# The low parts of the first 56 weight tiles: GpSimd subtracts, where ScalarE negated and a DMA added

## The chip, the cores and the metric

The kernel runs on one core of one Trainium2 chip. The metric is the device time of one execution, in microseconds (us). A core has five engines with a program each: TensorE (PE; its weight loads are listed as PEld), VectorE (DVE), ScalarE (ACT), GpSimd (POOL) and SyncE (SP), which here only issues DMAs. Sixteen DMA engines are shared by all queues: q1 holds what SP issues, q0 what POOL issues.

## What is computed

The reference is a stack of four layers on a sequence of 512 tokens of width 1024, in float32: a convolution beside an RWKV recurrence, a sparse attention, a gated linear recurrence, and a full attention. Only the first lines of the first layer matter here:

```python
mod = cond @ ada_w[l] + ada_b[l]
shift, scale, gate = jnp.split(mod, 3, axis=-1)
h = rms_norm(x, norm_g[l]) * (1.0 + scale[:, None, :]) + shift[:, None, :]
z = h @ even_w_in[j]
a_val, a_glu, a_gate, r, k, v, wd, ad, b_gate = split_cols(z, EVEN_SIZES)
```

## The kernel before

**Products in three parts.** Every float32 weight w and every activation x is written as a high part in TensorE's fp32r format and a low part, the rest. A product is then three matmuls (`mm3`, lines 168 to 170): high weight by high activation, high weight by low activation, low weight by high activation. In the profile the tiles are `wr` (raw weights as loaded), `wh` and `wl` (their high and low parts); the high and low parts of the activations are both called `h`.

**How a weight is split.** `wparts` takes up to four weight tiles of 128x128 at once. ScalarE casts them into `wh` (L145) and writes their negative, rounded to fp32r, into `wl` (L146); then a DMA on POOL's queue adds the raw weights to `wl` (L147), reading and writing SBUF. The rounded negative is minus the high part, so what is left is the low part. `wr` has three buffers, `wh` and `wl` have four each.

**The first stage, called START here.** The layer begins with seven column blocks (`START`: one of each kind of output) that go through all eight input blocks k = 0 to 7 together, each in its own PSUM bank, so that the work can begin with the first input block. `wrows` (L150) loads the seven weight tiles of one k in one DMA (L155, 448 KB) and calls `wparts` twice, with four tiles and with three. That is 8 x 7 = 56 tiles, 16 calls, and nothing else calls `wrows`. Each k is 7 x 3 = 21 matmuls of 512 columns.

**The modulation beside it.** The scale and shift of two input blocks at a time come from `ada_first`, 2 MB for each pair of blocks, loaded by SP (L434) into two buffers, `AR` and `BK`. `columns` multiplies and adds it on DVE (L445, L447: eight instructions), four small matmuls sum over partitions (L450), DVE adds the bias (L453, L428), scales x (L501) and ScalarE and DVE make the two parts of `h` (L332, L333). So the matmuls of k = 2, 4 and 6 wait for an L450 group that stands in PE's own order.

**After START** come single column blocks (`project`, `wsplit`), the convolution's taps on DVE (L859, 216 instructions), and two loops over eight chunks of the recurrence (`chunk`, `ahead`), in which ScalarE copies (L733, L739, L750, L772) stand between small matmuls.

**The order** of each engine's instructions is set when the kernel is built: a scheduler runs a model of the timeline over the whole program and writes each engine's list. SP's DMAs are a list of their own and start in that order; eight semaphores go round among them, so that a DMA also waits for the one eight before it.

Of the kernel before, what the change touches and what calls it, by code (L numbers as in the profile page):

```python
# [10 lines left out]
F = mybir.dt.float32  # L11
# [4 lines left out]
OP = mybir.AluOpType  # L16
# [36 lines left out]
class Ctx:  # L53
# [84 lines left out]
            out += [(h[:, i], l[:, i]) for i in range(n)] if rows else [[z.rearrange("p a c -> p (a c)") for z in (h, l)]]  # L138
        return out

    def wparts(self, raw, tag=None):

        nc, n = self.nc, raw.shape[1]
        h, l = ((self.t(tag, (P, 4, P), R) if tag else self.wp.tile([P, 4, P], R, name=self.name(z), tag=z, bufs=4))[:, :n] for z in ("wh", "wl"))
        nc.scalar.copy(h, raw)  # L145
        nc.scalar.mul(l, raw, -1.0)  # L146
        nc.gpsimd.dma_start(out=l, in_=raw, accum_op=OP.add)  # L147
        return h, l

    def wrows(self, key, ct, k):  # L150

        nc = self.nc
        raw = self.wp.tile([P, 8, P], F, name=self.name("wr"), tag="wr", bufs=3)
        n, d = len(ct), ct[1] - ct[0]
        nc.sync.dma_start(out=raw[:, :n], in_=self.ins[key][ct[0]:ct[-1] + 1:d, :, k].rearrange("c p n -> p c n"))  # L155
        out = []
        for o in (0, 4):
            m = min(4, n - o)
            h, l = self.wparts(raw[:, o:o + m])
            out += [(h[:, i], l[:, i]) for i in range(m)]  # L160
        return out

# [1500 lines left out]
```

## Time and profile before

| | |
|---|---|
| median of 3 runs | 1786.72 us (1777.45 to 1789.82) |
| the profiled execution | 1791.05 us, its span 1789.3 us |
| busy in the span | PE 1657.9 us, DVE 1142.2, ACT 1090.4, POOL 637.6 |
| mean granted TensorE clock | 0.955 of full speed |

The times in the rows count from the start of the span. "Granted clock" is the share of full speed that TensorE was given. An idle time in brackets behind a row is that of the engine just before it, with what ended it.

### The profile page before, as it was taken

To read this page: it belongs to the slowest core of one execution; us is meant where nothing else is said; L and a number is where in the kernel's file an instruction comes from. 1 tells how busy PE (TensorE), PEld (TensorE's weight loads), DVE (VectorE), ACT (ScalarE), POOL (GpSimd) and SP (SyncE) were. 2 spreads that over 40 slices of the span, in tenths; PEclk is the share of its full clock that TensorE was granted. 3 is DMA by queue.
4 is the path that set the end of the run, shared out by engine and by line. 5 is a ranking of instruction groups with operands and counts; after the bars stand their busy time and mean duration, and the time that the engine had idled before them with its cause. 6 is when DMAs were issued, how large, how long until landed. Compare 5 with 4: busy or idle time off the path is not lost.

```text
span 1789.3 us, 26544 instructions
## 1 busy us (share of the span) xinstructions
PE 1657.9 (93%) x9250; PEld 1310.1 (73%) x9250; DVE 1142.2 (64%) x2247; ACT 1090.4 (61%) x2106; POOL 637.6 (36%) x678
## 2 busy tenths in 40 slices
PE   5899999998995999888999899999999999999997
PEld 4676777776664777767887688888788777877775
DVE  6489776795948567456968878922688621454442
ACT  3574545445554435478565678765789755776775
POOL 1244423233566212133323445332333333333332
PEclk9899997898998989899999999999999999999999
DMA  9866894446678976476879741078777798865654
GB/s 284 211 147 163 184 215 110 107 95 174 153 179 193 273 219 151 119 170 142 179 168 229 197 89 35 18 166 193 165 177 167 150 190 190 199 143 138 154 109 116
DMA packets 164087, 289.19 MB, mean 162 GB/s; under 512 B 43985, under 2 KB 60753, under 8 KB 162929
## 3 DMA queue, kind: packets, MB, share of 16 engines
q0 software_dynamic: 60352, 107.24, 35.7%
q1 hardware_dynamic: 99568, 172.91, 30.9%
q10 hardware_dynamic: 4032, 7.34, 1.1%
q8 instruction: 73, 1.20, 0.3%
q14 instruction: 62, 0.50, 0.1%
HBM read 162.10 MB, written 18.12 MB: 101 GB/s over the span
## 4 chain that ended last, share of the span: by engine, by line
PE 59%; DVE 13%; DMA 12%; issue 8%; ACT 3%; POOL 3%; SPq 1%; POOLq 0%; DVEq 0%; ACTq 0%
PE ps L168 15%; PE ps L169 15%; PE ps L170 15%; DVE x L859 4%; DMA wl<-wr 3%; DMA wr<-in_even_w_in 2%; POOL wl L147 1%; DMA adm<-in_ada_w 1%; PE ps L1525 1%; PE ps L729 1%; DMA sp<-gt 1%; PE ps L1521 1%; PE ps L550 1%; PE ps L1261 1%; POOL mean L894 1%
## 5 line engine op out<-in xcount | busy, mean ns | idle before, releaser
L147 POOL DMA_DIRECT2D wl<-wr x416 | 364.7, 882 | 871.6 <-ACT wl L146 772.3
L170 PE MATMUL ps<-h,wl 128*128 128x512 f32 x1240 | 498.8, 406 | 29.4 <-DMA wl<-wr 29.0
L168 PE MATMUL ps<-h,wh 128*128 128x512 f32 x1240 | 508.5, 415 | 18.7 <-ACT h L332 6.8
L169 PE MATMUL ps<-h,wh 128*128 128x512 f32 x1240 | 500.0, 405 | 0.1
L145 ACT CAST wh<-wr 128x512 fp32r<-128x512 f32 (+1 forms) x416 | 251.9, 606 | 355.6 <-PE ps L169 253.8
L170 PEld LDWEIGHTS ps<-h,wl 128*128 128x128 f32 x1240 | 241.0, 195 | 91.0 <-DMA wl<-wr 37.5
L168 PEld LDWEIGHTS ps<-h,wh 128*128 128x128 f32 x1240 | 243.4, 197 | 83.3 <-ACT h L332 8.3
L169 PEld LDWEIGHTS ps<-h,wh 128*128 128x128 f32 x1240 | 242.0, 195 | 52.7 <-issue 2.7
L146 ACT ACTIVATE wl<-wr 128x512 fp32r<-128x512 f32 (+1 forms) x416 | 256.5, 617 | 28.0 <-PE ps L169 26.5
L859 DVE SCALAR_TENSOR_TENSOR x<-cu,vec,x 128x512 f32<-128x512 f32 x216 | 185.9, 862 | 4.9
L1258 POOL TENSOR_SCALAR pp<-pp,st 128x512 f32<-128x512 f32 x32 | 52.2, 1632 | 68.9 <-DVE st L1254 58.8
L1253 ACT ACTIVATE pp<-pp,st 128x512 f32<-128x512 f32 x64 | 46.2, 722 | 18.2 <-DVE st L1252 18.0
L1515 DVE CUSTOM_DVE_ANT_0 pp<-ps,nb 128x128 f32<-128x128 f32 (+3 forms) x64 | 30.6, 488 | 30.3 <-PE ps L1510 21.8
L169 PE MATMUL ps<-wl,h 128*128 128x512 f32 x120 | 47.6, 398 | 0.7 <-DMA wl<-wr 0.7
L1252 DVE CUSTOM_DVE_ANT_0 pp<-ps,bias 128x512 f32<-128x512 f32 x64 | 43.6, 681 | 6.4 <-PE ps L1261 6.0
L170 PE MATMUL ps<-wh,h 128*128 128x512 f32 x120 | 46.5, 393 | 0.0
L688 DVE TENSOR_TENSOR q<-q,q 128x112 f32<-128x112 f32 (+25 forms) x108 | 27.2, 288 | 29.2 <-DMA q<-sp 28.8
L168 PE MATMUL ps<-wh,h 128*128 128x512 f32 x120 | 45.4, 405 | 0.0
L288 ACT CAST pT<-ps 128x512 fp32r<-128x512 f32 x64 | 36.4, 577 | 14.1 <-PE ps L1261 13.6
L1518 POOL TENSOR_SCALAR pp<-pp,st 128x128 f32<-128x128 f32 (+1 forms) x32 | 32.0, 1032 | 36.5 <-DVE st L1517 36.4
L289 DVE TENSOR_TENSOR pT<-ps,pT 128x512 fp32r<-128x512 f32 x64 | 43.3, 680 | 0.8 <-ACT pT L288 0.7
L1188 DVE MATCH_REPLACE8 acc<-m,acc 128x512 f32<-128x512 f32 x64 | 42.8, 674 | 0.0
(522 smaller groups left out, 3332.1 us busy)
## 6 DMA issues: line engine op xcount, KB each, us to landing
wl<-wr POOLq DMA_DIRECT2D x376, 256.0 KB, 4.1
wr<-in_even_w_in SPq DMA_DIRECT2D x50, 512.0 KB, 4.1
wr<-in_odd_w_in SPq DMA_DIRECT2D x39, 512.0 KB, 4.2
wr<-in_lru_w_in SPq DMA_DIRECT2D x24, 512.0 KB, 3.8
wr<-in_fox_w_qkg SPq DMA_DIRECT2D x24, 512.0 KB, 4.4
k<-in_ada_w SPq DMA_DIRECT2D x32, 256.0 KB, 3.9
wr<-in_odd_w_out SPq DMA_DIRECT2D x16, 512.0 KB, 4.0
wl<-wr POOLq DMA_DIRECT2D x40, 192.0 KB, 4.1
```

The lines of the kernel that those rows point to most:

```text
L145: nc.scalar.copy(h, raw)
L146: nc.scalar.mul(l, raw, -1.0)
L147: nc.gpsimd.dma_start(out=l, in_=raw, accum_op=OP.add)
L168: mm(ps, lhsT=w[0], rhs=x[0], start=first, stop=False)
L169: mm(ps, lhsT=w[0], rhs=x[1], start=False, stop=False)
L170: self.last_mm = mm(ps, lhsT=w[1], rhs=x[0], start=False, stop=last).ins
L289: nc.vector.tensor_tensor(out=l, in0=src, in1=h.bitcast(F), op=OP.subtract)
L859: nc.vector.scalar_tensor_tensor(out=acc, in0=u[:, q:q + S], scalar=w[q], in1=acc, op0=OP.mult, op1=OP.add)
L1188: nc.vector.match_replace(out=acc, in_to_replace=m8, in_values=acc, imm_value=TAKEN)
L1252: nc.vector.tensor_tensor_reduce(out=pp, in0=lg, in1=bias[t], scale=1.0, scalar=3e38, op0=OP.add, op1=OP.min, accum_out=mx)
L1253: nc.scalar.activation(pp, pp, AF.Exp, scale=-1.0, bias=mx, accum_out=sm)
L1258: (nc.vector if t % 2 else nc.gpsimd).tensor_scalar(out=pp, in0=pp, scalar1=sm, scalar2=None, op0=OP.mult)
```

## The change

`wparts` gets a switch `sub`, and `wrows` sets it. For START's 16 calls ScalarE's negative and the adding DMA go; POOL subtracts the high part from the raw weights in one instruction. All other weights are split as before.

```diff
-    def wparts(self, raw, tag=None):
+    def wparts(self, raw, tag=None, sub=False):
...
         nc.scalar.copy(h, raw)
-        nc.scalar.mul(l, raw, -1.0)
-        nc.gpsimd.dma_start(out=l, in_=raw, accum_op=OP.add)
+        if sub:
+            nc.gpsimd.tensor_tensor(out=l, in0=raw, in1=h.bitcast(F), op=OP.subtract)
+        else:
+            nc.scalar.mul(l, raw, -1.0)
+            nc.gpsimd.dma_start(out=l, in_=raw, accum_op=OP.add)
         return h, l
...
-            h, l = self.wparts(raw[:, o:o + m])
+            h, l = self.wparts(raw[:, o:o + m], sub=True)
```

Lines from 142 on stand one to four lower in the kernel after. The scheduler's order changes with it, in START and in the two chunk loops; from the second layer's first blocks on it is the same. Three places follow.

On PE at the end of k = 1 the matmuls of the low parts stand like this before (`wl42` and `wl44` are the low weights of k = 1, `ps65` is the L450 group for k = 2 and 3, `wh49` the high weights of k = 2):

```order
L169 MATMUL ps33_148<-h63_249,wh43_171 128x512
L450 MATMUL ps65_261<-ones_73,SAV64_252 128x1 x4
L170 MATMUL ps27_142<-h62_248,wl42_167 128x512
L170 MATMUL ps28_143<-h62_248,wl42_167 128x512
L170 MATMUL ps29_144<-h62_248,wl42_167 128x512
L170 MATMUL ps30_145<-h62_248,wl42_167 128x512
L170 MATMUL ps31_146<-h62_248,wl44_172 128x512
L170 MATMUL ps32_147<-h62_248,wl44_172 128x512
L170 MATMUL ps33_148<-h62_248,wl44_172 128x512
L168 MATMUL ps27_142<-h78_318,wh49_197 128x512
```

and like this after:

```order
L174 MATMUL ps32_147<-h62_240,wl44_169 128x512
L172 MATMUL ps33_148<-h62_240,wh43_168 128x512
L173 MATMUL ps33_148<-h63_241,wh43_168 128x512
L454 MATMUL ps65_253<-ones_73,SAV64_244 128x1 x4
L174 MATMUL ps33_148<-h62_240,wl44_169 128x512
L172 MATMUL ps27_142<-h78_306,wh49_193 128x512
```

Before, seven matmuls stand between the small group and the step that waits for it; after, one (behind k = 3 none; behind k = 5 none either way).

On SP, the loads of START's later weights and of `ada_first`, before:

```order
L103 DMA inv1031_5599<-in_inv 128x4
L434 DMA AR66_289<-in_ada_first 128x2048 x2
L155 DMA wr53_207<-in_even_w_in 128x7x128
L434 DMA BK85_386<-in_ada_first 128x2048 x2
L155 DMA wr67_292<-in_even_w_in 128x7x128
L155 DMA wr72_304<-in_even_w_in 128x7x128
```

and after:

```order
L103 DMA inv1031_5583<-in_inv 128x4
L159 DMA wr53_201<-in_even_w_in 128x7x128
L438 DMA AR66_281<-in_ada_first 128x2048 x2
L159 DMA wr67_284<-in_even_w_in 128x7x128
L438 DMA BK85_374<-in_ada_first 128x2048 x2
L159 DMA wr72_294<-in_even_w_in 128x7x128
```

The weights of k = 3 and k = 4 (`wr53`, `wr67`) go ahead of the 2 MB loads beside them.

On ACT in the first chunk loop (`q4480` and `BKt` are made for a later chunk, `U468` belongs to the running one, `wh493` and `wl494` to a filling weight block), before:

```order
L750 COPY BKt452_2501<-ps451_2496 128x512
L145 CAST wh493_2727<-wr492_2725 128x512
L146 ACTIVATE wl494_2728<-wr492_2725 128x512
L772 COPY U468_2588<-ps467_2579 128x256
L739 COPY SAV479_2658<-ps483_2676 64x256 x2
L783 COPY SAV445_2469<-ps476_2624 64x256
L733 COPY q4480_2661<-AR161_779 64x4x64 x2
```

and after:

```order
L754 COPY BKt452_2485<-ps451_2480 128x512
L737 COPY q4480_2645<-AR161_763 64x4x64
L776 COPY U468_2572<-ps467_2563 128x256
L737 COPY q4480_2645<-AR161_763 64x4x64
L146 CAST wh493_2711<-wr492_2709 128x512
L150 ACTIVATE wl494_2712<-wr492_2709 128x512
L743 COPY SAV479_2642<-ps483_2660 64x256 x2
```

The copies for the later chunk moved forward, and the filling weights behind `U468`.

## Rows read from the trace of the kernel before

**Rows 1.** Windows: busy us of each engine (instructions), granted clock, DMA share, GB/s.

```profile
40.00:60.00 20.00, 11.78 (x42) 8.20 (x41) 6.65 (x12) 5.94 (x12) 3.68 (x5) 0.83 0.96 258
...
220.00:260.00 40.00, 37.12 (x161) 29.38 (x160) 27.56 (x119) 17.74 (x33) 11.18 (x13) 0.96 0.97 225
```

**Rows 2.** Chain of waits, 0 to 100 us: start, length, what.

```profile
38.11 16.50 DMA wr<-in_even_w_in
...
63.07 6.32 DMA wr<-in_even_w_in
```

**Rows 3.** SP's own waits, 0 to 100 us: total, times, longest.

```profile
SPq L155 <- DMA wl<-wr: 21.4, 3, 10.7
```

**Rows 4.** DMA queues, 0 to 80 us: packets, MB, share of 16 engines.

```profile
q1 hardware_dynamic: 11360, 17.09, 64.9%
q0 software_dynamic: 2304, 3.67, 27.0%
```

**Rows 5.** Timeline of PE in START: start, length, instruction, idle time before it.

```profile
25.27 3.23 PE L168 MATMUL ps<-h,wh 128*128 128x512 f32 x7 [2.36 <-ACT h L332]
...
34.68 0.95 PE L450 MATMUL ps<-ones,SAV 128*128 128x1 f32 x8
35.49 1.88 PE L170 MATMUL ps<-h,wl 128*128 128x512 f32 x7
37.62 1.89 PE L168 MATMUL ps<-h,wh 128*128 128x512 f32 x7 [0.25 <-ACT h L332]
...
44.74 1.63 PE L170 MATMUL ps<-h,wl 128*128 128x512 f32 x4 [3.65 <-DMA wl<-wr]
48.29 0.80 PE L168 MATMUL ps<-h,wh 128*128 128x512 f32 x1 [1.92 <-ACT wh L145]
...
59.83 1.89 PE L168 MATMUL ps<-h,wh 128*128 128x512 f32 x7 [1.62 <-ACT h L332]
...
64.72 1.75 PE L168 MATMUL ps<-h,wh 128*128 128x512 f32 x7
66.31 0.39 PE L169 MATMUL ps<-h,wh 128*128 128x512 f32 x1
...
72.43 3.24 PE L168 MATMUL ps<-h,wh 128*128 128x512 f32 x7 [1.99 <-ACT h L332]
...
84.90 0.39 PE L168 MATMUL ps<-h,wh 128*128 128x512 f32 x1
```

**Rows 6.** ScalarE's negatives by shape, 0 to 85 us: busy, mean ns.

```profile
L146 ACT ACTIVATE wl<-wr 128x512 fp32r<-128x512 f32 x10 | 6.2, 624 | 0.0
```

**Rows 7.** POOL's groups by shape, whole span: busy us, mean ns.

```profile
L864 POOL TENSOR_TENSOR pa<-pa,awa 128x512 f32<-128x512 f32 x16 | 25.4, 1589 | 15.2 <-ACT awa L863 14.9
...
L1365 POOL TENSOR_TENSOR wal<-wax,wah 128x256 fp32r<-128x256 f32 x12 | 11.3, 946 | 13.7 <-ACT wah L1364 13.7
...
L972 POOL TENSOR_TENSOR h<-k,h 128x512 fp32r<-128x512 f32 x4 | 5.6, 1538 | 0.0
```

**Rows 8.** Timeline of DVE in START.

```profile
27.09 5.47 DVE L447 SCALAR_TENSOR_TENSOR SAV<-BK,cs,SAV 128x512 f32<-128x512 f32 x7
...
37.60 1.42 DVE L333 SCALAR_TENSOR_TENSOR h<-s,mod,h 128x512 fp32r<-128x512 f32 x2
```

**Rows 9.** Chain of waits, 175 to 185 us: start, length, what.

```profile
177.85 0.76 DVE x L859
178.63 1.68 DVE x L859
```

**Rows 10.** Timeline of POOL at the same place, and at 537 us.

```profile
177.91 1.84 POOL L864 TENSOR_TENSOR pa<-pa,awa 128x512 f32<-128x512 f32 x1 [1.93 <-ACT awa L863]
...
537.26 12.65 POOL L894 TENSOR_TENSOR mean<-mean,cu 128x512 f32<-128x512 f32 x1
```

**Rows 11.** ScalarE's copies of the chunk loops by shape, whole span.

```profile
L733 ACT COPY q<-AR 64x256 f32<-64x256 f32 x32 | 13.0, 405 | 32.6 <-DVE q L731 32.5
...
L750 ACT COPY BKt<-ps 128x512 f32<-128x512 f32 x14 | 8.1, 580 | 4.6 <-PE ps L748 3.1 <-PE ps L790 1.3
```

## The prediction

> **What bounds the kernel now.** Four views, in this order. *The stretch by windows* shows where the touched work lies: between 40 and 60 us TensorE is busy 11.8 of 20 us at a granted clock of 0.83, while the DMA engines are 96% busy [rows 1]. START is the one long stretch of this kernel in which TensorE starves for data. *The chain of waits* says on what: it runs through loads of raw weights, one of 16.5 us and one of 6.3 us [rows 2]. *SyncE's own waits* say why those loads are late: 21.4 us in all it waits for adding DMAs before it may overwrite a raw buffer [rows 3]. *The DMA queues* give the other half of the reason: up to 80 us q0 moves 3.67 MB, just the 56 tiles of 64 KB, and fills the 16 engines for 27.0% of 80 us, which is 21.6 us; the loads in q1 fill 64.9%, 51.9 us [rows 4]. The adding DMAs thus take a quarter of the engines' time in a stretch where they are the scarce thing, and hold back the loads a second time through the buffers.
>
> What START costs on TensorE can be read from its timeline [rows 5]. It runs from 25.27 to 84.90 us, 59.6 us. One matmul at full clock takes (66.31 - 64.72) / 7 = 0.227 us, so its 8 x 21 = 168 matmuls need 38.1 us. Three small groups L450 inside it take 35.49 - 34.68 = 0.81 us each, 2.4 us. The five idle times in the rows come to 0.25 + 3.65 + 1.92 + 1.62 + 1.99 = 9.4 us. What is left, 9.7 us, is TensorE at its lower level (1.2 GHz), as in the first seven matmuls (3.23 us for what takes 1.89 at full clock), and shorter waits.
>
> **The change part by part.**
>
> *Removed from ScalarE:* 16 negatives, 0.62 us for a full one [rows 6], some 9 us in all. ScalarE is busy 5.9 of 20 us there [rows 1]; the gain is nothing by itself. It shortens the way from a landed weight to its low part by half a microsecond, which only matters where TensorE waits for that.
>
> *Removed from the DMA engines:* 21.6 us of their time. Nothing else needs q0 there. The loads, alone, need 51.9 us of engine time in 80 us, and SyncE may issue each as soon as POOL's subtract has read the buffer. Then the last of START's weights can land by about 52 us, and the step that needs it (k = 7) cannot start before 68 us in the sum below: the loads leave the path, with some 15 us to spare. The new order on SyncE helps: the weights of k = 3 and 4 no longer stand behind 2 MB of modulation weights. Those come later by one load of 448 KB, about a microsecond, against the two steps (9.5 us) that DVE has for them.
>
> *Added on POOL:* 16 subtracts. The same instruction on 128x512 with an fp32r result takes 1.54 us (L972), on 128x256 0.95 us (L1365) [rows 7]; halfway, 1.24 us, for 128x384. Per k that is 2.8 us against 21 x 0.227 = 4.8 us of matmuls, and 22 us in all where POOL is otherwise nearly idle. So POOL keeps up. The bounds: 0.95 us as if width cost nothing, and 1.84 us, the slowest of the like in rows [rows 10]; at 1.84 us, 3.7 us a step, it still keeps up.
>
> *Moved on TensorE:* the low-part matmuls of k = 1 and 3 come before the small group and no longer behind it. Before, seven of them filled the time in which DVE and ScalarE made the next `h`, and the wait behind them was 0.25 us; now only one does, or none. The bare wait is the one before k = 6, where nothing stood behind the group: 1.99 us [rows 5]. So k = 2, 4 and 6 each wait 2.0 us, 6.0 us in all.
>
> *The floor of START after:* 38.1 + 2.4 + 6.0 us, and 1.3 us for the first seven matmuls at the lower level (3.23 - 1.89), are 47.8 us. From 25.27 us it ends at 73.1, 11.8 us earlier than before. The start itself I leave: it hangs on the modulation of the first two blocks and on ScalarE's casts of a weight that lands at the same time as before.
>
> *Two costs on top of the floor.* First the clock. Of two waits of about the same length, the one of 1.62 us was followed by seven matmuls in 1.89 us, the one of 1.99 us by seven in 3.24 us [rows 5]. So each of the three waits may cost 0 or 1.35 us more, 0 to 4.1 us; I take half, 2.0 us, since the waits lie at the longer of the two but the rows have one of each. Second, POOL against DVE. A subtract on POOL beside a DVE instruction with two inputs in SBUF slows one of them: the DVE instruction that began 0.72 us after POOL's L864 took 1.68 us where its neighbour took 0.76 [rows 9, 10], so 0.92 us lost; in another place POOL lost, and one instruction took 12.65 us beside a dense run of DVE work [rows 10]. In START POOL's loss is harmless, since a low part is needed last in its step. DVE's counts where it is on the path: at the start (the four subtracts of k = 0 and 1 lie there, beside the first modulation and the first `h`), and in the chain to `h` of k = 2, 4, 6. The runs of L447 are covered: seven take 5.5 us and the `h` before them 1.4 us [rows 8], against 9.5 us of matmuls, so two lost times of 0.92 us fit into the rest. I count three of the sixteen subtracts on the path, 2.8 us; the bounds are none, 0, and all sixteen, 14.7 us.
>
> The Trainium skill (SBUF — State Buffer, section "SBUF: two separate sides") says that DVE and GpSimd share one port pair as an exclusive lock and that the loser blocks for the other's whole instruction. The rows show a loser in both directions, but DVE lost 0.92 us of a 1.84 us instruction; by the page three meetings would cost about 3 x 1.4 = 4.2 us, an estimate from the page's rule, and the kernel would be some 1.4 us slower than in my sum.
>
> *The sum:* 11.8 - 2.0 - 2.8 = 7.0 us. What comes after START is a chain of matmuls and DVE work that begins with START's results, so it shifts as a whole; where the DMA engines fill up again (97% at 220 to 260 us, [rows 1]) the loads are released by that same work. In the chunk loops the new order moves copies of 0.405 us (L733) and 0.580 us (L750) before or behind the copy U that the chain needs; there are 14 of the latter [rows 11], so at the outside 14 x 0.985 = 13.8 us, of either sign. The rows shown have instances moved both ways, and TensorE has filling matmuls there; I take zero, and 4 us either way for the range.
>
> The profiled execution is 1791.05 us, 1789.3 of it the span, so it would become 1784. It lies 4.3 us above the median of the three runs, of which the predicted time is 1786.7 - 7.0 = 1779.7, say **1780 us**.
>
> **The rivals.**
>
> *POOL's subtracts hold up DVE on the path.* For it: the 1.68 us row; sixteen subtracts and 28 instructions L447 lie in the same 50 us. Against it: most L447 have slack, and POOL may be the loser. Price 0.92 us each, on the 9.8 us that the floor and the clock leave; from eleven of the sixteen on the path the kernel is slower than before. All sixteen: 1786.7 - 9.8 + 14.7 = 1791.6 us, slower.
>
> *The gain is given back behind START.* If a transfer or a buffer in the first layer, and not START's end, sets when the chunk loop starts, nothing is left: 1787 us. For it: the DMA engines at 97% at 220 to 260 us. Against it: what fills them there is triggered by the shifted work.
>
> *Full clock, no lock, and loops that gain.* 11.8 us in START and two thirds of the outside figure of the loops, 9 us, give 1766 us. For it: in the piece of order shown, a cast and a negative of a weight, about 0.6 us each [rows 6], no longer stand before U. Against it: further copies do.
>
> *The loops lose.* With the first rival and all 13.8 us against it, 1805 us. Against it: it needs every chunk on ScalarE's side of the chain.
>
> That the change doesn't do what it says, the loads staying on the path because POOL is starved: a subtract as slow as the 12.65 us row would hold one raw buffer for 11 us, as the worst wait of 10.7 us did before; once, this costs no more than what the loads have to spare. It falls into the second rival.
>
> **How the numbers follow.** Forecast, a gain of 3 to 12 us: 0.59. First rival, between 3 us faster and 5 slower: 0.14. Given back: 0.11. Faster loops: 0.11. Slower loops: 0.05. One per cent is 17.9 us, about what a measurement of this kernel can tell from no change; three runs of before lay 12.4 us apart. Only the third rival is beyond it on the fast side, 0.11, and only the last on the slow side, 0.05; the rest is 0.84. The range goes down to the third rival's edge, 1767, and up to just over the first rival's worst, 1793, which leaves about 2 in 10 outside.
>
> **What the profile after would show.** Right: no q0 traffic before START's end; no wait of TensorE for `wl` or `wh` in START; three waits for `h` of about 2 us before k = 2, 4, 6; START's last matmul at about 78 us; the first L859 of DVE about 7 us earlier than before, and the same shift at the first chunk and at the layer's end. Wrong in the lock: L447, L501 or L333 of 1.7 us in the chain, or POOL's subtracts far above 1.5 us with TensorE waiting for them. Wrong in the carrying: START ends earlier and the layer doesn't. The forecast as a whole fails if the loads still stand on the chain of waits after 50 us, or if the chunk loops change by more than START.

## The result, and the profile after

| | before | after |
|---|---|---|
| median | 1786.35 us, 10 executions (1777.45 to 1791.34) | 1774.13 us, 10 executions (1760.81 to 1777.31) |
| the profiled execution | 1791.05 us, span 1789.3 | 1774.27 us, span 1772.5 |
| busy in the span | PE 1657.9, DVE 1142.2, ACT 1090.4, POOL 637.6 us | PE 1655.6, DVE 1144.7, ACT 1082.0, POOL 638.8 us |
| mean granted clock | 0.955 | 0.960 |

The ratio is 0.9931, with an interval of 0.9906 to 0.9956: 12.2 us faster, 5.9 us under the forecast of 1780 and inside its range.

START first. DMA queues of after, 0 to 80 us (as in [rows 4]): q0, which took 27.0%, has no line any more. Its first packets move at 80.4 us, for weights that stand behind START.

```profile
q1 hardware_dynamic: 11360, 17.09, 63.0%
```

SyncE's own waits, 0 to 100 us: START's loads waited 21.4 us for adding DMAs [rows 3], now 11.6 us for subtracts. The loads of the weights behind START (L133) wait for START's subtracts too.

```profile
SPq L133 <- POOL wl L148: 17.7, 3, 10.6
SPq L159 <- POOL wl L148: 11.6, 2, 7.8
```

Timeline of POOL: two subtracts that run alone, one of each width.

```profile
37.75 1.29 POOL L148 TENSOR_TENSOR wl<-wr,wh 128x512 fp32r<-128x512 f32 x1 [1.07 <-ACT wh L146]
...
53.63 0.99 POOL L148 TENSOR_TENSOR wl<-wr,wh 128x384 fp32r<-128x384 f32 x1 [0.65 <-ACT wh L146]
```

Timeline of PE in START (as in [rows 5]). The last line is START's last matmul, the 168th from the first. Before, the 168th stood at 84.68 us; the one at 84.90 us, to which the prediction counts, is one too far.

```profile
27.59 3.35 PE L172 MATMUL ps<-h,wh 128*128 128x512 f32 x7 [2.09 <-ACT h L336]
...
38.85 0.94 PE L454 MATMUL ps<-ones,SAV 128*128 128x1 f32 x8
39.66 0.48 PE L174 MATMUL ps<-h,wl 128*128 128x512 f32 x1
41.79 3.35 PE L172 MATMUL ps<-h,wh 128*128 128x512 f32 x7 [1.65 <-ACT h L336]
...
56.24 3.35 PE L172 MATMUL ps<-h,wh 128*128 128x512 f32 x7 [2.27 <-ACT h L336]
...
71.92 2.90 PE L172 MATMUL ps<-h,wh 128*128 128x512 f32 x7 [2.27 <-ACT h L336]
...
82.96 0.39 PE L174 MATMUL ps<-h,wl 128*128 128x512 f32 x1
```

The only idle times longer than 0.15 us in START are the three before k = 2, 4 and 6. Each is followed by seven matmuls that take 2.9 to 3.4 us in place of 1.9. The windows of after show why (columns as in [rows 1]); the line in the middle is a stretch without a wait:

```profile
41.80:45.30 3.50, 3.50 (x9) 2.79 (x10) 3.30 (x6) 0.72 (x1) 0.03 (x1) 0.52 1.01 418
45.30:53.00 7.70, 7.70 (x35) 6.37 (x34) 5.91 (x6) 1.76 (x3) 4.51 (x3) 1.00 0.64 190
...
56.20:62.30 6.10, 6.06 (x14) 4.79 (x15) 5.87 (x9) 0.65 (x1) 0.00 (x0) 0.50 0.18 68
...
71.90:75.90 4.00, 3.98 (x11) 3.11 (x11) 1.50 (x2) 1.10 (x2) 0.00 (x0) 0.57 0.27 102
```

START is 55.4 us long (27.59 to 82.96) where it was 59.4 (25.27 to 84.68). The chain of waits of after, 15 to 30 us, shows what stands ahead of it: two of VectorE's modulation steps, 0.68 us each when alone, lie beside the first two subtracts (POOL at 19.11 us).

```profile
18.43 0.68 DVE SAV L451
...
19.14 1.80 DVE SAV L451
20.96 1.36 DVE SAV L451
```

The first L863 of VectorE (L859 before, at 85.03 us), by its timeline:

```profile
82.93 0.75 DVE L863 SCALAR_TENSOR_TENSOR x<-cu,vec,x 128x512 f32<-128x512 f32 x1
```

So START hands on 2.1 us, not 7, between these two executions. They are 16.8 us apart. The same VectorE instruction stands at 282.3 us in both, 5.0 us earlier at 507 us (507.29 and 502.33), and 10.2 us at 623 us (623.20 and 612.96). In these two executions, then, most of the difference arose far behind the edited code, where only the order had changed. How far two single executions can be trusted is the first question of the experiments.

### The profile page after: what moved, and what is told of

Its sections match the earlier page's. It is cut to its first block, busy times and chain, and to the rows that moved or that the text cites. A ratio compares the mean times of both kernels' runs of the same rounds, so it can differ in the third digit from the quotient of the medians.

```text
span 1772.5 us, 26499 instructions
## 1 busy us (share of the span) xinstructions
PE 1655.6 (93%) x9250; PEld 1310.6 (74%) x9250; DVE 1144.7 (65%) x2247; ACT 1082.0 (61%) x2090; POOL 638.8 (36%) x678
## 4 chain that ended last, share of the span: by engine, by line
PE 60%; DVE 15%; DMA 10%; issue 8%; ACT 3%; POOL 3%; SPq 1%; POOLq 0%; ACTq 0%; DVEq 0%
PE ps L172 16%; PE ps L173 15%; PE ps L174 15%; DVE x L863 5%; DMA wl<-wr 4%; POOL wl L151 2%; DMA adm<-in_ada_w 1%; PE ps L733 1%; PE ps L1529 1%; PE ps L1525 1%; PE ps L1265 1%; PE ps L554 1%; DVE pp L1256 1%; DVE pT L293 1%; PE ps L1510 1%
## 5 line engine op out<-in xcount | busy, mean ns | idle before, releaser
L151 POOL DMA_DIRECT2D wl<-wr x400 | 351.7, 882 | 824.1 <-ACT wl L150 704.2
L172 PEld LDWEIGHTS ps<-h,wh 128*128 128x128 f32 x1240 | 242.9, 196 | 89.2 <-DVE s L532 10.6
L150 ACT ACTIVATE wl<-wr 128x512 fp32r<-128x512 f32 (+1 forms) x400 | 247.6, 619 | 29.0 <-PE ps L173 27.3
L863 DVE SCALAR_TENSOR_TENSOR x<-cu,vec,x 128x512 f32<-128x512 f32 x216 | 186.0, 864 | 4.8
```

The lines of the kernel that those rows point to most:

```text
L172: mm(ps, lhsT=w[0], rhs=x[0], start=first, stop=False)
L863: nc.vector.scalar_tensor_tensor(out=acc, in0=u[:, q:q + S], scalar=w[q], in1=acc, op0=OP.mult, op1=OP.add)
```

## The experiments

Each kernel is the kernel before or after with one edit; the first has none. Every ratio is to the kernel before, run beside the one in question (medians of 1784.60 to 1784.71 us; 1786.35 in the table above). In START's table further down, first and last matmul are read from the timeline of PE of each.

**The kernel before once more** (one execution, 1783.25 us).

> The kernel before once more, unchanged, for a second trace. If the 10.9 us for which TensorE waits at 554.9 us, behind a GpSimd addition of 12.65 us, belongs to the order of the instructions, it stands here again at the same place, 8 to 12 us long, and the stretches from 620 us to the end differ from the first trace by less than 2 us. If it is chance of one execution, it is gone or under 4 us here, and the time comes out near 1778 us.

The wait stands again, and the GpSimd addition that is caught is the same one, the sixth of seven. Waits of PE, 500 to 640 us, and the timeline of POOL:

```profile
PE ps L170 <- DMA wl<-wr: 10.9, 1, 10.9
```

```profile
539.91 12.68 POOL L894 TENSOR_TENSOR mean<-mean,cu 128x512 f32<-128x512 f32 x1
```

The other half failed: from the VectorE instruction at 623.20 us of the first trace to the one at 701.19, the first took 78.0 us, this one 71.8 (628.04 to 699.79). Two executions of one program differ by 6 us in one stretch, so a difference of that size between single traces proves nothing. The first L859, 85.03 us in the first trace, stands at 87.30 us here.

**Same number of subtracts, two orders.** The scheduler's order behind START depends on which k subtract, in a way that can be used: these four kernels have four or twelve subtracting calls, each number with both orders. (Each kernel has one of the four added lines.)

```diff
-            h, l = self.wparts(raw[:, o:o + m], sub=True)
+            h, l = self.wparts(raw[:, o:o + m], sub=k in (1, 3, 4, 5, 6, 7))   # twelve, order of before
+            h, l = self.wparts(raw[:, o:o + m], sub=k < 2)                      # four, order of after
+            h, l = self.wparts(raw[:, o:o + m], sub=k >= 6)                     # four, order of before
+            h, l = self.wparts(raw[:, o:o + m], sub=k < 6)                      # twelve, order of after
```

Twelve, order of before:

> Subtract for k = 1, 3, 4, 5, 6 and 7, twelve of the sixteen calls; the scheduler then leaves everything behind START in the order of the kernel before. Theory of the forecast (the gain is START's and is carried through): START ends 2 us or more earlier, the shift stays to the end, 1776 to 1779 us. Theory of the order (START's gain is given back by 230 us, and the new order behind START makes the gain): 1783 to 1790 us, no difference to before, and the wait of some 10 us behind the GpSimd addition at about 550 us is there.

Four, order of after:

> Subtract for k = 0 and 1 alone, four of the sixteen calls; the scheduler then orders everything behind START as in the kernel after. Theory of the forecast: a quarter of the gain, 1782 to 1786 us. Theory of the order: nearly the whole gain of 12 us, 1771 to 1778 us, no wait of some 10 us behind a GpSimd addition at about 550 us.

Four, order of before:

> Subtract for k = 6 and 7 alone, four of the sixteen calls as in the run with k = 0 and 1 (1770.2 us), but here the scheduler leaves everything else in the order of the kernel before. Theory of the order: no gain, 1782 to 1789 us; in the trace, 64 to 69 us from the end of VectorE's dense run (about 557 us) to the addition that stands at 623 us in the trace of before, where the two runs with the new order took 53 to 57. Rival, the dose (what matters is that some subtracts take DMAs away, and k = 0 and 1 were the lucky ones): 1770 to 1778 us.

Twelve, order of after:

> Subtract for k = 0 to 5, twelve of the sixteen calls as in the run with the old order (1785.2 us), but with the whole order of the kernel after. Theory of the order: 1768 to 1777 us, and 52 to 58 us from the end of VectorE's dense run to the addition at 623 us. Rival, the dose: 1782 to 1788 us as the other run with twelve. START: 54 to 57 us long, as in the kernel after, if the order in it matters more than the number of subtracts; 58 to 60 us if not.

| | order of before | order of after |
|---|---|---|
| 4 subtracts | 1779.42 us, 0.9975 (0.9952 to 0.9998) | 1770.21 us, 0.9917 (0.9891 to 0.9943) |
| 12 subtracts | 1785.15 us, 0.9992 (0.9968 to 1.0015) | 1774.50 us, 0.9946 (0.9922 to 0.9970) |

At the same number of subtracts the kernels with the new order are 9.2 and 10.7 us faster. At the same order, going from four to twelve gains nothing (5.7 and 4.3 us slower). The theory of the forecast, a gain in proportion to START's subtracts, falls: twelve subtracts with the old order are no faster than before. One rival these four kernels leave open: both with the new order subtract for k = 0 and 1, and neither with the old order does so for both. What that does in START is in the table further down (START ends 2.4 and 3.0 us earlier with the new order, so some 7 and 8 us lie behind it); that it does no more than that, no run tests. The run with four and the old order was 2.6 us faster than I had put the lower end; from the end of VectorE's dense run to the addition at 623 us it took 59.2 us (564.46 to 623.68), where the theory of the catch wanted 64 to 69.

And in both kernels with the old order the wait of 10.9 us was gone, against expectation. Waits of PE, 500 to 640 us, with twelve subtracts and with four:

```profile
PE ps L174 <- DMA wl<-wr: 0.8, 1, 0.8
...
PE ps L174 <- DMA wl<-wr: 0.3, 1, 0.3
```

The timeline of POOL with twelve subtracts and the old order, at the same additions, the sixth and the seventh:

```profile
534.21 1.56 POOL L898 TENSOR_TENSOR mean<-mean,cu 128x512 f32<-128x512 f32 x1
...
537.12 1.59 POOL L898 TENSOR_TENSOR mean<-mean,cu 128x512 f32<-128x512 f32 x1
...
545.76 8.13 POOL L976 TENSOR_TENSOR h<-k,h 128x512 fp32r<-128x512 f32 x2
```

There VectorE lost (its timeline, a pair that takes 0.38 us alone), and later GpSimd instructions were caught, the pair in the last line above. Alone such a pair takes 2.8 us; in after it is caught too, for 7.96 us.

```profile
533.65 2.21 DVE L693 TENSOR_TENSOR q<-q,q 128x87 f32<-128x87 f32 x2
```

**Old order in the first chunk loop alone.** Two edits give the same order behind START: that of before up to 458 us, that of after from there.

```diff
-            h, l = self.wparts(raw[:, o:o + m], sub=True)
+            h, l = self.wparts(raw[:, o:o + m], sub=k >= 4)
```

> Subtract for k = 4 to 7, eight of the sixteen calls; the scheduler then keeps the order of the kernel before up to 458 us, the first chunk loop included, and takes that of the kernel after from there (458 to 526 us and the second chunk loop). Theory of the forecast: half the gain, 1779 to 1782 us. Theory of the order, if the stretch from 458 to 526 us is what matters (the additions on GpSimd then end before the dense run on VectorE): 1773 to 1779 us. If the first chunk loop's order matters: 1780 to 1787 us.

```diff
+            h, l = self.wparts(raw[:, o:o + m], sub=o == 4)
```

> Subtract in the second call of every k (three of its seven tiles), so eight of the sixteen calls; behind START the scheduler gives the same order as in the run with k = 4 to 7 (1780.8 us): that of the kernel before up to 458 us, that of the kernel after from there. If the first chunk loop's order is part of the gain, 1778 to 1784 us again. If that run was chance and only the order from 458 us on matters, 1770 to 1777 us. START: 57 to 61 us, as with the other kernels in which k = 0 to 5 still have adding DMAs.

1780.80 us, 0.9980 (0.9953 to 1.0007), and 1780.84 us, 0.9987 (0.9960 to 1.0013). The order from 458 us on gains little or nothing by itself; the rest, 6 to 11 us against the three kernels with the whole new order (1774.13, 1770.21, 1774.50), hangs on the order up to 458 us, START included. START's end is not what sets it: the kernel with k = 4 to 7 and the one with k = 0 and 1 end START at 85.06 and 85.24 us and are 10.6 us apart in the median.

**START in the kernels that differ in their subtracts:**

| kernel | first matmul | last | length |
|---|---|---|---|
| before, and once more | 25.27, 27.89 us | 84.68, 86.94 | 59.4, 59.1 us |
| k = 6, 7 (old order) | 26.17 | 87.66 | 61.5 |
| k = 1, 3 to 7 (old order) | 27.04 | 86.17 | 59.1 |
| k = 4 to 7; second calls | 26.32; 26.89 | 85.06; 88.09 | 58.7; 61.2 |
| k = 0, 1 | 27.33 | 85.24 | 57.9 |
| k = 0 to 5 | 27.55 | 83.13 | 55.6 |
| after | 27.59 | 82.96 | 55.4 |

**Additions moved from GpSimd to VectorE**, to take the catch away: the last one in the kernel before (`i == ND - 1`), the last two in before, the last two in after. The order from 569 to 623 us changes with it.

```diff
-                    nc.gpsimd.tensor_tensor(out=acc, in0=acc, in1=sq[:, :S], op=OP.add)
+                    (nc.vector if i >= ND - 2 else nc.gpsimd).tensor_tensor(out=acc, in0=acc, in1=sq[:, :S], op=OP.add)
```

> The kernel before with nothing changed in START; the last of the seven GpSimd additions that stand before VectorE's dense run (the one of 12.65 us) is made by VectorE. The order is that of before up to there, and another one from 569 to 623 us. If that addition, which holds the weights' DMAs behind it, is what the old order costs: no wait of 10.9 us at about 555 us, 8 to 12 us less from 507 to 623 us, and 1774 to 1779 us. Rival (the wait only covers others that come in its place): under 4 us less there, and 1781 to 1787 us.

> The kernel before, with the last two of the seven GpSimd additions made by VectorE (with one moved: 1776.0 us, and the one that was then last on GpSimd was caught for 6.55 us and TensorE waited 4.8). Theory (a GpSimd instruction caught in VectorE's dense run holds the weights' DMAs): no addition above 2.5 us, no wait of TensorE for low weights above 2 us between 530 and 560 us, 1770 to 1777 us. Rival (the other order from 569 to 623 us that comes with the edit made the gain of the run with one moved): no difference to it, 1774 to 1778 us, whatever the waits do.

> The kernel after, with the same two additions made by VectorE. In the trace of after no addition is caught. If the gain of the change is mostly that of not being caught, this is 1770 to 1776 us, the same as after, and within 4 us of the kernel before with the two moved: with the catch out of both, the change itself is worth what START brings, 1 to 4 us. If START and the first chunk loop are worth what the forecast said, it is 7 us or more below the kernel before with the two moved, 1764 to 1770 us.

Before with one moved: 1775.97 us, 0.9955 (0.9933 to 0.9977); with two: 1773.46 us, 0.9948 (0.9922 to 0.9974). After with two: 1763.13 us, 0.9873 (0.9840 to 0.9906). This is the fastest kernel of the study, 11.0 us below after's median above and 21.5 below that of before beside it (1784.62). The edit is worth about the same in both kernels (11.2 and 11.0 us), and with it the change is still worth 10.3 us. (The 11.0 is between two batches; by the ratios to before it is about 10.) So what this edit takes away is not what the change had taken away. The first of the three expectations has one thing wrong: the addition of 12.65 us is the sixth, not the last, so with only the last moved it stayed on GpSimd. It was caught for 6.55 us, and the wait for low weights shrank to 4.8 us. The timeline of POOL, before and with one moved:

```profile
550.47 1.55 POOL L894 TENSOR_TENSOR mean<-mean,cu 128x512 f32<-128x512 f32 x1
...
536.31 6.55 POOL L894 TENSOR_TENSOR mean<-mean,cu 128x512 f32<-128x512 f32 x1
```

With two moved no addition was caught. In after no addition had been caught in the first place; its waits of PE, 500 to 640 us, show four others in their place:

```profile
PE ps L172 <- ACT fg L879: 4.2, 2, 3.7
PE ps L774 <- DVE SAV L800: 3.2, 1, 3.2
PE ps L172 <- DVE k L968: 3.2, 1, 3.2
PE ps L752 <- DVE q L735: 2.8, 1, 2.8
```

Where the edit acts in after is told by the windows of 560 to 625 us: of after, then of after with two moved.

```profile
560.00:625.00 65.00, 58.74 (x568) 46.47 (x568) 40.46 (x59) 33.46 (x64) 15.34 (x17) 0.84 0.92 260
```

```profile
560.00:625.00 65.00, 62.07 (x656) 50.28 (x657) 44.53 (x72) 34.16 (x67) 15.81 (x18) 0.90 0.99 283
```

TensorE is busy 3.3 us more there and has issued 88 matmuls more. The matmuls differ in size, so the count is only a sign that the work stands earlier. Whether the additions or the order that comes with them did that, these runs don't separate.

**The catch put back into after:**

```diff
+                    for _ in range(3 if i == ND - 2 else 0):
+                        nc.gpsimd.tensor_scalar(out=sq[:, :S], in0=sq[:, :S], scalar1=1.0, scalar2=None, op0=OP.mult)
                     nc.gpsimd.tensor_tensor(out=acc, in0=acc, in1=sq[:, :S], op=OP.add)
```

> The kernel after with three more GpSimd instructions ahead of the addition before the last (each multiplies one square by 1.0, some 1 us alone), so that GpSimd still has such work when VectorE's dense run goes. Theory: one or more of them is caught for 5 to 13 us, the low weights' DMAs behind it come as late, TensorE waits 5 to 11 us for them at about 545 us, and the kernel loses most of its gain: 1779 to 1787 us. Rival (GpSimd's work there is off the path): within 3 us of after, 1771 to 1777 us.

One of the three was caught, as the timeline of POOL shows:

```profile
528.76 11.44 POOL L899 TENSOR_SCALAR cu<-cu 128x512 f32<-128x512 f32 x1
```

The time is 1773.64 us, 0.9936 (0.9910 to 0.9961), the same as after, as the rival had it. But the catch brought no wait for low weights: TensorE's longest wait there is 4.2 us, for GpSimd's `h`. And the order of several engines from 527 us on changed with the edit. So a kernel with a catch of 11 us can be as fast as after; what a wait of 10.9 us costs, this run does not measure.

**Fillers behind the small group in START:**

```diff
+            if i % 2 and i < 7:
+                for p, w in zip(pss, ws[i]):
+                    mm(p, lhsT=w[0], rhs=hT[i][0], start=False, stop=False)
+                    hi = mm(p, lhsT=w[0], rhs=hT[i][1], start=False, stop=False).ins
+                with K.tc.issue_after(hi):
+                    small = A.columns(i + 1, raw[i + 1], K.last_l)   # now returns its last matmul
+                with K.tc.issue_after(small):
+                    for p, w in zip(pss, ws[i]):
+                        mm(p, lhsT=w[1], rhs=hT[i][0], start=False, stop=False)
+                continue
```

> The kernel after, with the seven matmuls of the low weights of k = 1, 3 and 5 behind the small group L454 and no longer before it, so that they run while the next h is made. In the trace of after START takes 55.4 us: 38.1 of matmuls at full clock, 2.4 of small groups, 6.2 of three waits for h, and 8.7 left, which I put down to TensorE's lower level (1.2 GHz) behind each wait. If that is right, the waits shrink to under 1.5 us in all and the lower level with them: START takes 44 to 48 us. Rival (VectorE's chain from one modulation to the next is the bound, so that the wait only moves to the small group): 50 to 55 us. The scheduler orders what lies behind START in a third way, so the whole time may be anything from 1762 to 1785 us.

START took 51.2 us (27.21 to 78.42): 4.2 shorter, but the rival's figure. The timeline of PE:

```profile
40.74 1.90 PE L172 MATMUL ps<-h,wh 128*128 128x512 f32 x7 [0.25 <-ACT h L336]
...
51.32 1.02 PE L454 MATMUL ps<-ones,SAV 128*128 128x1 f32 x8 [2.29 <-DVE SAV L451]
52.20 2.54 PE L516 MATMUL ps<-h,wl 128*128 128x512 f32 x7
...
64.89 1.02 PE L454 MATMUL ps<-ones,SAV 128*128 128x1 f32 x8 [1.29 <-DVE SAV L451]
```

The first wait is filled as meant (0.25 us, and full clock behind it). The other two move to the small group, which now waits for VectorE's modulation, and the lower level follows them. The whole kernel takes 1790.71 us, 1.0027 (1.0000 to 1.0055), no faster than before, 16.6 us slower than after and outside what I had given. The order behind START is a third one, in which TensorE stands idle for 15.6 us ahead of L727, with no releaser that the profile shows, and waits 11.7 us for low weights (waits of PE, 500 to 640 us):

```profile
PE ps L727 <- issue: 15.6, 1, 15.6
PE ps L174 <- DMA wl<-wr: 11.7, 3, 9.0
```

## Why the prediction came out where it did

The time was forecast well, but by luck: two terms were wrong in opposite directions. By the last of its own signs ("if the chunk loops change by more than START") the forecast as a whole failed.

*The removed DMAs and waits: right,* but for q0, which is not silent to START's end (82.96 us): it moves weights of the next blocks from 80.4 us on. No wait of TensorE for `wl` or `wh`, and no load in the chain of waits between START's first matmul and its last.

*POOL keeps up: right.* A subtract takes 1.29 us alone and 0.99 for 128x384, against the 1.54 and 1.24 assumed.

*Three bare waits for `h`, 6.0 us in all: right*, 1.65 + 2.27 + 2.27 = 6.2.

*VectorE against GpSimd, 2.8 us on the path: nearly.* On the chain lie the two slow steps ahead of the first matmul, 1.80 + 1.36 - 2 x 0.68 = 1.8 us. Whether START begins later by it isn't shown: its first matmul stands at 27.59 us in after, and at 25.27 and 27.89 us in the two traces of before.

*The clock, "1.3 us for the first seven" and "2.0 us" for the rest: this step failed.* At the lower level (1.2 GHz) two matmuls begin 0.43 us apart and not 0.227. Counting such steps in the timeline of PE, START lost 7.5 us to them before and 8.5 after, on some 40 matmuls each. I had put the 9.7 us that were left over in before down to the lower level and shorter waits (the waits in START come to 11.1 us, 1.7 more than the five rows) and then let nearly all of it vanish with the waits for weights. But the new waits were followed by the lower level as old ones had been, and each costs 1.7 to 2.9 us for 8 to 14 matmuls, not 1.35 for seven: 38.1 + 2.4 + 6.2 + 8.5 = 55.2 us, where 55.4 were measured. START's term was 7.0 us; it measured 2.1 or 4.4 at the first L863, and 1.7 or 4.0 at the last matmul, by which of the two traces of before it is held against.

*Full carry-through: not shown.* At 282 us the two profiled executions stand level. Single traces differ there by more than this shift.

*"I take zero" for the chunk loops: this step failed too.* The pairs with equal numbers of subtracts differ by 9.2 and 10.7 us; with 2.4 and 3.0 us of that at START's end, some 7 to 8 of the 12 us are left for what lies behind START. The bound, 13.8 us, held. The price by ScalarE's copies on either side of U gave no sign, and no run here shows that those copies are what gains. What the runs show is nearest to the third rival, loops that gain, though its reason (a cast and a negative out of the way of U) is not shown; it came with START's clock at the lower level and so at the forecast's time.

*What stays open:* which instruction of the new order makes the gain. It hangs on the order up to 458 us; but in the traces the stretch from the VectorE instruction at 277.5 us of before to the one at 424.8 took 144 to 149 us with the old order (four traces) and 144 to 147 with the new (three), which is no difference. From the instruction at 507 us to the one at 623, the five kernels with the new order from 458 us on took 107 to 111 us and the four traces with the old order 114 to 118; but from there to 701 us they took 76 to 79, and the old order 72 to 73 (78 in the first trace of before), which gives most of it back. The gain is in the medians of ten to twelve executions and in no one stretch of single traces, and a trace may not stand for its kernel: the one of k = 0 and 1 is the slowest of its ten executions (1779.88 us), the one of k = 0 to 5 the second slowest of twelve (1781.22). The most visible candidate, the addition of 12.65 us that the prediction had in its rows [rows 10], is excluded as the whole: it is not caught in the traces of two kernels with the old order, one as slow as before and one 5 us faster, and a kernel with such a catch put back is as fast as after.

## What to carry to other kernels

Where a scheduler sets the order, an edit's own stage and the order that it causes behind it are two effects, and the second can be the larger: look for edits of other sizes that leave the order as it was, or change it alone, and compare medians, not traces. When waits of TensorE are exchanged for others, the time at its lower level can come back with them, as it did behind all three waits here: count the matmuls that step by 0.43 us in place of 0.227 before claiming what is left over. Fillers behind a small group took START's first wait away and shortened START by 4.2 us, but the other two waits moved to the next groups, which waited for VectorE, and the whole kernel, with yet another order behind START, was slower.

## What the runs showed of the hardware that was not expected

Who loses when GpSimd and VectorE meet is not decided by the order of the program. The same addition, the sixth, in the same order of instructions, took 12.65 and 12.68 us in two executions of before and 1.56 us with twelve subtracts, where VectorE lost instead: the pair of 128x87 took 2.21 us, 1.8 more than alone. The Trainium skill (SBUF — State Buffer, section "SBUF: two separate sides") says that whichever of the two starts first holds the shared ports for its whole instruction. VectorE's loss agrees with that, 1.8 us being about the length of the addition; a GpSimd instruction that stands blocked for 12 us beside VectorE instructions of about 0.25 us each is more than one instruction's wait.

The record of the granted clock missed the lower level at START's beginning. The windows of after:

```profile
27.60:31.80 4.20, 4.20 (x10) 3.32 (x11) 4.06 (x7) 0.61 (x1) 0.00 (x0) 1.00 0.76 223
```

Ten matmuls took 4.2 us there, as at half clock, and the record says 1.00; the steps between matmuls are the surer sign.

Executions of one kernel spread by 11 to 23 us, and the mean granted clock goes with the time, without its being shown which sets which: with twelve subtracts and the old order 1777.09 us at 0.962, and 1792.33 us at 0.955.
